# A decoder layer on one core: sums of weight tiles moved from VectorE to adding DMAs, and the work of T1 put first

## The chip, the cores and the metric

The kernel runs on one core of one Trainium2 chip. The metric is device time in microseconds, the median of the runs. The engines are TensorE (PE: matmuls and, as PEld, weight loads), VectorE (DVE), ScalarE (ACT), GpSimd (POOL) and SyncE (SP). Each runs its own list of instructions in order and waits for the others by semaphores. DMAs are issued here from SP's queue and POOL's; a DMA issued by POOL can add what it moves to what stands at the destination.

## The reference

One layer of a decoder trunk (DEPTH is 1, so the mixer is the pooling one): a norm, multi-scale causal pooling with a blockwise projection, a residual, a norm, and a gated feed-forward with a causal convolution of three taps. All in float32, sequence 1024, width 1024, hidden width 2816.

```python
def conv_ffn(x, w_in, conv_w, conv_b, w_out):
    h = causal_depthwise_conv(x @ w_in, conv_w, conv_b)
    val, gate = jnp.split(h, 2, axis=-1)
    return (jax.nn.silu(gate) * val) @ w_out

    h = rms_norm(x, norm_mix_g[layer])
    y = pool_mixer(h, pool_w[j], pool_b[j], pool_scale[j])
    x = x + y
    x = x + conv_ffn(rms_norm(x, norm_ffn_g[layer]), ...)
```

## The kernel before

**Stages.** First the mixer: eight tiles j of 128 rows are normed, pooled by matmuls (`psd`), projected (`psy`) and added to x. Each tile is normed again (`n2`), turned by TensorE in eight transposes (`pst`) and becomes a column block of the operands of the feed-forward. The second stage multiplies by `w_in`: 22 tiles n of 128 hidden units of the value and 128 of the gate. The third multiplies by `w_out`. It is not touched.

**Seven products instead of eight.** Both matrix products are done on two by two blocks with seven block products and some sums. For `w_in` one side is the weight tile `win` (blocks a11, a12, a21, a22), the other the turned rows (b11 to b22, kept in `n2f`). From the tile come S3 = a11 + a21, S1 = a21 + a22, S2 = a11 + S1 and S4 = a12 + S2, each in place of a block but S3, which has a buffer of its own. From the rows come T1 = b11 - b12, T3 = b22 - b12, T2 = -b22 - T1 and T4 = b22 - b21 + T1. The products are P1 = A11 B11, P2 = A12 B21, P5 = S1 T1, P3 = S4 B22, P6 = S2 T2, P7 = S3 T3, P4 = A22 T4.

**High and low parts.** Every operand is split: ScalarE rounds it into a high part (line 76 for weight tiles, line 311 for the rows' operands) and VectorE subtracts that from the source for the remainder (lines 77 and 312). A block product is twelve matmuls 128x512: for each of four slices of depth high by high, high by remainder, remainder by high. So the first matmul needs only the high parts, the second the rows' remainder too. The splits of one operand T2, T3, T4 or B22 come in two halves.

**Banks.** P1 and P2 of a tile add up in a bank X, P5 and P3 in a bank Z, and P6, P7 and P4 in a bank Y. Between them VectorE reads the bank: q2 after P6 (line 401), hb after P7 (line 409: r less Y), and hb's other half after P4 (line 414). r is read from Z after P5 (line 406). P4 may only add into Y once hb has been read. After P4 come the convolutions of value and gate (lines 419 to 421), a Silu and a product, and g goes to DRAM.

**Order.** The program is written as a list of events (n, P); while event k runs, the splits of event k + 5 are issued (`prep_event`). Tiles 0 and 1 take part in the mixer's last steps: P1 and P2 there, then P5, P3, P6, P7, P4. A scheduler places the instructions on each engine by its own estimates, with `tc.issue_after` as a constraint. The load of weight tile n + 2 (line 320) is issued once A22 of tile n is split. The sums of tiles 0 and 1 are made by POOL's adding DMAs (line 334), those of all later tiles by VectorE (lines 350 to 358).

## Time and profile before

| | |
|---|---|
| median of 3 runs | 704.09 us (703.36 to 705.65) |
| the profiled execution | 702.61 us, of which the span is 700.9 |
| TensorE busy | 693.9 us, 3154 matmuls |
| VectorE busy | 600.5 us |
| ScalarE busy | 343.2 us |
| GpSimd busy | 12.5 us |
| first matmul of P5 of tile 0 | 78.55 us |
| first matmul of P6 of tile 0 | 90.06 us |

In the profile's rows a tile has its name without its number (S is S3's buffer, T any of T1 to T4, B any of B11, B21, B22). A row of the timeline gives the start in the span, the length, the engine, the line, the operation, what is written and read, and the idle time before it with what ended it. A busy share is an average over the span: what a stage is worth is read from that stage.

### The profile page before, as it was taken

How to read it: one execution, taken by the hardware profiler on the slowest of the kernel's cores; microseconds unless marked ns; L12 is line 12 of the kernel's file. 1: busy time of each engine (PE TensorE's matmuls, PEld its weight loads, DVE VectorE, ACT ScalarE, POOL GpSimd, SP SyncE). 2: the span in 40 equal slices, each digit the busy share in tenths (PEclk: the TensorE clock that was granted, in tenths of full speed). 3: DMA queues.
4: the chain of work that ended last, by engine and by line, in shares of the span. 5: the costliest groups of instructions: out<-in, count | busy, mean ns of one | idle time of the engine just before them, and what ended most of it. 6: DMA issues, size and time to landing. Idle time of an engine off the chain costs nothing.

```text
span 700.9 us, 8493 instructions
## 1 busy us (share of the span) xinstructions
PE 693.9 (99%) x3154; PEld 573.7 (82%) x3154; DVE 600.5 (86%) x885; ACT 343.2 (49%) x515; POOL 12.5 (2%) x30
## 2 busy tenths in 40 slices
PE   8999999999999999999999999999999999999998
PEld 5898778888888888888888888888888888888886
DVE  5688999999888888888988888876887988999985
ACT  4786545454444444444545454454554444444431
POOL 3110000000000000000000000000000000000000
PEclk9999999999999999999999999999999999999999
DMA  9854112232222112222222212229989700122131
GB/s 307 302 141 121 57 65 91 89 122 91 67 84 74 60 78 90 91 90 91 91 90 91 86 65 91 91 84 338 335 305 335 277 22 1 61 90 87 64 106 60
DMA packets 32555, 85.47 MB, mean 122 GB/s; under 512 B 3689, under 2 KB 5377, under 8 KB 29698
## 3 DMA queue, kind: packets, MB, share of 16 engines
q1 hardware_dynamic: 31296, 82.82, 32.8%
...
q8 instruction: 24, 0.39, 0.2%
...
## 4 chain that ended last, share of the span: by engine, by line
PE 96%; DVE 2%; DMA 1%; ACT 1%; issue 0%; ACTq 0%; DVEq 0%
PE oP L723 30%; PE Y L372 26%; PE Z L372 17%; PE X L372 16%; PE psy L259 3%; PE psd L180 2%; DMA bias_hl<-rows_raw 1%; PE pst L292 1%; PE psy L262 1%; DVE n2f L323 0%; DMA x<-in_x_dram 0%; DVE T L312 0%; PE ps_edges L180 0%; PE ps_gain L227 0%; DVE n L277 0%; DVE S4s L77 0%
## 5 line engine op out<-in xcount | busy, mean ns | idle before, releaser
L723 PE MATMUL oP<-oBP,oAP 128*128 128x512 f32 (+1 forms) x924 | 208.8, 388 | 0.0
L723 PEld LDWEIGHTS oP<-oBP,oAP 128*128 128x128 f32 x924 | 172.9, 188 | 36.0 <-DVE oBP L77 0.3
L372 PE MATMUL Z<-T,S1s 128*128 128x512 f32 x264 | 64.0, 390 | 1.4 <-ACT T L311 1.2
L372 PE MATMUL X<-B,A11s 128*128 128x512 f32 x264 | 64.3, 390 | 0.0
L372 PE MATMUL Y<-T,S2s 128*128 128x512 f32 x264 | 64.0, 390 | 0.0
L372 PE MATMUL X<-B,A12s 128*128 128x512 f32 x264 | 63.5, 389 | 0.0
L372 PE MATMUL Y<-T,S3s 128*128 128x512 f32 x264 | 63.4, 389 | 0.0
L372 PE MATMUL Y<-T,A22s 128*128 128x512 f32 x264 | 63.4, 389 | 0.0
L372 PE MATMUL Z<-B,S4s 128*128 128x512 f32 x264 | 63.2, 389 | 0.0
L372 PEld LDWEIGHTS Z<-T,S1s 128*128 128x128 f32 x264 | 49.3, 188 | 12.6 <-ACT T L311 1.6
L372 PEld LDWEIGHTS Y<-T,S2s 128*128 128x128 f32 x264 | 49.4, 188 | 10.8 <-ACT S2s L76 0.4
L372 PEld LDWEIGHTS Y<-T,S3s 128*128 128x128 f32 x264 | 49.5, 188 | 10.3
L372 PEld LDWEIGHTS Z<-B,S4s 128*128 128x128 f32 x264 | 49.5, 188 | 10.3
L372 PEld LDWEIGHTS Y<-T,A22s 128*128 128x128 f32 x264 | 49.5, 188 | 10.3
L372 PEld LDWEIGHTS X<-B,A12s 128*128 128x128 f32 x264 | 49.5, 188 | 10.2
L372 PEld LDWEIGHTS X<-B,A11s 128*128 128x128 f32 x264 | 49.4, 188 | 10.2
L76 ACT ACTIVATE oBP<-blk 128x512 fp32r<-128x512 f32 x53 | 33.5, 633 | 49.1 <-PE oP L723 32.2
L77 DVE TENSOR_TENSOR oBP<-blk,oBP 128x512 fp32r<-128x512 f32 x53 | 36.6, 691 | 13.3 <-ACT oBP L76 13.3
L430 ACT ACTIVATE gate<-gate 128x1024 f32<-128x1024 f32 x22 | 23.3, 1061 | 44.5 <-DVE gate L421 44.5
L76 ACT ACTIVATE oAP<-blk 128x512 fp32r<-128x512 f32 x55 | 34.1, 621 | 19.2 <-DVE blk L323 15.9
L326 DVE TENSOR_TENSOR win<-win 128x512 f32<-128x512 f32 x60 | 41.3, 688 | 1.1
L77 DVE TENSOR_TENSOR oAP<-blk,oAP 128x512 fp32r<-128x512 f32 x55 | 37.7, 685 | 2.6 <-ACT oAP L76 2.6
(128 smaller groups left out, 941.4 us busy)
## 6 DMA issues: line engine op xcount, KB each, us to landing
win<-in_w_in_dram SPq DMA_DIRECT2D x22, 1024.0 KB, 4.8
...
```

Of the source, the lines that this page charges most:

```text
L76: nc.scalar.activation(t[:, 0, :], src, AF.Copy)
L77: m = nc.vector.tensor_tensor(t[:, 1, :], src, t[:, 0, :].bitcast(F32), ALU.subtract)
L180: m = nc.tensor.matmul(ps[:, c * P : (c + 1) * P], src[:, c * P : (c + 1) * P], weights[:, c // 2, :], start=True, stop=True)
L259: nc.tensor.matmul(o, dh[:, c, :], wps[:, c, :], start=c % 4 == 0, stop=False, skip_group_check=True)
L262: m = nc.tensor.matmul(ps[:, cols], ones, bias_hl[:, cols], start=False, stop=True, skip_group_check=True)
L292: nc.tensor.transpose(ps[:, c * P : (c + 1) * P], n2[:, c * P : (c + 1) * P], ident)
L326: nc.vector.tensor_tensor(out, a, b, ALU.add)
L372: nc.tensor.matmul(bank, a[:, i, ks], b[:, l, k, :], start=opens and m == 0, stop=m == 11, skip_group_check=not opens)
L430: nc.scalar.activation(gate, gate, AF.Silu)
L723: nc.tensor.matmul(bank, a[:, u, i * P : (i + 1) * P], b[:, v, c], start=opens and first, stop=g == NP2 - 1 and m == 2, skip_group_check=n ...
```

## The change

- T4's sum with T1 and the four sums of weight tiles 2, 3 and 4 are done by adding DMAs of POOL (`more`, `sums_in`, LATER_SUMS). A DMA from DRAM first fills S3's buffer with a11. T4's two adds move 512 KB each, the others 256 KB.
- The transposes of a row tile (`ffn_turn`) are apart from what is made of it (`ffn_operand`, `ffn_last`). For tiles 6 and 7 T1 is made first and T4's difference (`ffn_last`) follows r of tile 0. The last transposes stand at a fixed place, after the third slice of P2 of tile 0 (`between`). The norm of tile 7 stands ahead of the subtractions of tile 6.
- A tile `lower` is taken first in the pool of Y and Z, so that Z lies in other banks. B22's splits and r are issued sooner. The splits of events 7 to 9 follow r, and those of events 14 and 15 are held back.

```diff
@@ -285,13 +285,21 @@
     for b in ("B11", "T1", "B21"):
         nops[b] = nop_tile(nop_a, b)
 
-    def ffn_operand(j):
+    turned = {}
+
+    def ffn_turn(j):
         n2 = n2s.pop(j)
         ps = bank2(f"pst{j}")
         for c in range(NK):
-            nc.tensor.transpose(ps[:, c * P : (c + 1) * P], n2[:, c * P : (c + 1) * P], ident)
-        cols = slice(j * P, (j + 1) * P)
-        ps3 = ps.rearrange("p (c s) -> p c s", c=NK)
+            m = nc.tensor.transpose(ps[:, c * P : (c + 1) * P], n2[:, c * P : (c + 1) * P], ident)
+        marks["turned"] = m.ins
+        turned[j] = ps.rearrange("p (c s) -> p c s", c=NK)
+        if j >= NS // 2:
+            nc.scalar.activation(n2f[:, 4:, j * P : (j + 1) * P], turned[j][:, 4:, :], AF.Copy)
+        return m.ins
+
+    def ffn_operand(j, last=True):
+        ps3, cols = turned[j], slice(j * P, (j + 1) * P)
         lo, hi = slice(0, 4), slice(4, 8)
         if j < NS // 2:
             split_n(nops["B11"], ps3[:, lo, :], cols)
@@ -299,17 +307,23 @@
             nc.scalar.activation(n2f[:, :, cols], ps3, AF.Copy)
             return
         cols0 = slice(cols.start - NH, cols.stop - NH)
-        b11, b12, b21, b22 = n2f[:, lo, cols0], ps3[:, lo, :], n2f[:, hi, cols0], n2f[:, hi, cols]
-        nc.scalar.activation(b22, ps3[:, hi, :], AF.Copy)
+        b11, b12, b22 = n2f[:, lo, cols0], ps3[:, lo, :], n2f[:, hi, cols]
+
         sub(b11, b11, b12)
-        split_n(nops["T1"], b11, cols0)
-        sub(n2f[:, lo, cols], b22, b12)
-        sub(b21, b22, b21)
+        m = sub(n2f[:, lo, cols], b22, b12)
+        if last:
+            m = ffn_last(j)
+        with tc.issue_after(m):
+            marks[f"T1_{j}"] = split_n(nops["T1"], b11, cols0)
+
+    def ffn_last(j):
+        b21, b22 = (n2f[:, 4:, t * P : (t + 1) * P] for t in (j - NS // 2, j))
+        return sub(b21, b22, b21)
 
     def split_n(t, src, cols=slice(None), ks=slice(None)):
         h = t[:, 0, ks, cols]
-        nc.scalar.activation(h, src, AF.Copy)
-        nc.vector.tensor_tensor(t[:, 1, ks, cols], src, h.bitcast(F32), ALU.subtract)
+        marks["split_hi"] = nc.scalar.activation(h, src, AF.Copy).ins
+        return nc.vector.tensor_tensor(t[:, 1, ks, cols], src, h.bitcast(F32), ALU.subtract).ins
 
 
     order = [j + k * NP2 for j in range(NP2) for k in range(2)]
...
 
+    def more(out, a):
+        nc.gpsimd.dma_start(out, a, accum_op=ALU.add)
+
     def sums_in(n, step):
-
-        def more(out, a):
-            nc.gpsimd.dma_start(out, a, accum_op=ALU.add)
 
         a11, a12, a21, a22 = (raws[n][:, i, k * NH : (k + 1) * NH] for i in range(2) for k in range(2))
         if step == 0:
@@ -339,9 +353,10 @@
             nc.sync.dma_start(s3, w_in[order[n]][:, 0, :NH])
             more(s3, a21)
             more(a21, a22)
-        else:
+        if step in (1, "S2"):
             sums[n, "S2"] = a11
             more(a11, a21)
+        if step in (1, "S4"):
             sums[n, "S4"] = a12
             more(a12, a11)
 
@@ -361,16 +376,28 @@
         else:
             src = {"A11": a11, "A12": a12, "S1": a21, "A22": a22, "S2": a11, "S4": a12}[op]
         aops[n, op] = split(src, f"{op}s_{n}")
+        if n in LATER_SUMS and op in ("A11", "A12"):
+            sums_in(n, {"A11": "S2", "A12": "S4"}[op])
+
+            if op == "A12" and n + 1 in LATER_SUMS:
+                sums_in(n + 1, 0)
         if op == "A22" and n + 2 < NF:
             load_in(n + 2)
-
-    def product(bank, a, b, opens):
-        m = 0
+            if n + 2 == LATER_SUMS[0]:
+                sums_in(n + 2, 0)
+
+    def product(bank, a, b, opens, between):
+
+        m, order = 0, nullcontext()
         for k in range(4):
             ks = slice(k * P, (k + 1) * P)
-            for i, l in ((0, 0), (0, 1), (1, 0)):
-                nc.tensor.matmul(bank, a[:, i, ks], b[:, l, k, :], start=opens and m == 0, stop=m == 11, skip_group_check=not opens)
-                m += 1
+            with order:
+                for i, l in ((0, 0), (0, 1), (1, 0)):
+                    last = nc.tensor.matmul(bank, a[:, i, ks], b[:, l, k, :], start=opens and m == 0, stop=m == 11, skip_group_check=not opens)
+                    m += 1
+            if between and k == 2:
+                with tc.issue_after(last.ins):
+                    order = tc.issue_after(between())
 
     STEPS = {
         "P1": ("A11", "B11", "X"), "P6": ("S2", "T2", "Y"), "P5": ("S1", "T1", "Z"), "P2": ("A12", "B21", "X"),
...
@@ -493,11 +523,21 @@
             mixer_window(j - 1)
         if 1 <= j - 2 < NS:
             mixer_out(j - 2)
-        if 0 <= j - 2 < NS:
-            with tc.issue_after(marks["dh1+"]):
-                ffn_norm(j - 2)
-        if 0 <= j - 4 < NS:
-            ffn_operand(j - 4)
+        if j == 9:
+            ffn_turn(5)
+            with tc.issue_after(marks[7]):
+                ffn_operand(5)
+            with tc.issue_after(marks["T1_5"]):
+                ffn_norm(7)
+        elif j == 10:
+            ffn_turn(6)
+        else:
+            if 0 <= j - 2 < NS:
+                with tc.issue_after(marks["dh1+"]):
+                    ffn_norm(j - 2)
+            if 0 <= j - 4 < NS - 1:
+                ffn_turn(j - 4)
+                ffn_operand(j - 4)
         if j in (4, 6):
             load_in(j // 2 - 2)
             sums_in(j // 2 - 2, 0)
@@ -506,8 +546,19 @@
                 prep_event(j - 5)
         if j in (7, 8):
             sums_in(j - 7, 1)
-        if j in (8, 10, 11):
-            event((8, 10, 11).index(j))
+        if j == 8:
+            with tc.issue_after(marks["n2_6"]):
+                prep_event(4)
+                prep_event(5)
+            event(0)
+        if j == 10:
+            event(1)
+        if j == 11:
+            event(2, between=lambda: ffn_turn(7))
+            with tc.issue_after(marks["n2_7"]):
+                ffn_operand(6, last=False)
+                with tc.issue_after(marks["T1_6"]):
+                    ffn_operand(7, last=False)
         with tc.issue_after(marks["edges"]):
             stat(j + 1)
             stat(j + 2)
@@ -515,19 +566,29 @@
     nop_b = ctx.enter_context(tc.tile_pool(name="nop_b", bufs=1))
     left = ctx.enter_context(tc.tile_pool(name="left", bufs=1))
     ps_yz = ctx.enter_context(tc.tile_pool(name="ps_yz", bufs=3, space=PSUM))
+
+    ps_yz.tile([P, NH], F32, tag="Y", name="lower")
     for b in ("T2", "T3", "B22", "T4"):
         nops[b] = nop_tile(nop_b, b)
-    for k in range(4, 4 + LOOK):
-        with tc.issue_after(marks[NS - 1]):
-            prep_event(k)
     s0, s1 = slice(0, NH), slice(NH, S)
     lo, hi = slice(0, 4), slice(4, 8)
     halves = [slice(0, 2), slice(2, 4)]
     t1, t3, b22, t4 = n2f[:, lo, s0], n2f[:, lo, s1], n2f[:, hi, s1], n2f[:, hi, s0]
-    event(3)
-    event(4)
+    with tc.issue_after(marks["T1_7"]), tc.issue_after(marks["split_hi"]):
+        prep_event(6)
+        for ks in halves:
+            m = split_n(nops["B22"], b22[:, ks], ks=ks)
+    with tc.issue_after(marks["turned"]):
+        event(3)
+    with tc.issue_after(m):
+        event(4, prep=False)
+    with tc.issue_after(marks["r_0"]):
+        for j in (6, 7):
+            ffn_last(j)
+        for k in range(7, 4 + LOOK + 1):
+            prep_event(k)
     for ks in halves:
-        split_n(nops["B22"], b22[:, ks], ks=ks)
+        more(t4[:, ks], t1[:, ks])
     event(5)
     event(6)
     for ks in halves:
@@ -537,13 +598,17 @@
     event(8)
     for ks in halves:
         split_n(nops["T3"], t3[:, ks], ks=ks)
+    prep_event(9 + LOOK)
     for ks in halves:
-        add(t4[:, ks], t4[:, ks], t1[:, ks])
         split_n(nops["T4"], t4[:, ks], ks=ks)
     mid.close()
     late_stack = ExitStack()
     late = late_stack.enter_context(tc.tile_pool(name="late", bufs=1, side="right"))
-    for k in range(9, len(events)):
+    event(9, prep=False)
+    event(10, prep=False)
+    with tc.issue_after(marks["val0"][0]), tc.issue_after(marks["val0"][1]):
+        prep_event(10 + LOOK)
+    for k in range(11, len(events)):
         event(k)
     late_stack.close()
 
```

On VectorE the piece from r of tile 0 (`r_0`) to the first remainder of T2 read so before (line 534 makes T2; names end in the tile's number and a buffer number):

```order
L406 TENSOR_TENSOR r_0_832<-q1_0_673,Z0_819 128x512
L77 TENSOR_TENSOR A22s_0_838<-win0_415,A22s_0_838 128x512
L77 TENSOR_TENSOR S2s_1_858<-win1_540,S2s_1_858 128x512
L534 SCALAR_TENSOR_TENSOR n2f_161<-n2f_161 128x2x512
L406 TENSOR_TENSOR r_1_856<-q1_1_741,Z1_843 128x512
L534 SCALAR_TENSOR_TENSOR n2f_161<-n2f_161 128x2x512
L312 TENSOR_TENSOR T2_783<-n2f_161,T2_783 128x1024
```

and reads so now:

```order
L435 TENSOR_TENSOR r_0_826<-q1_0_679,Z0_813 128x512
L337 TENSOR_TENSOR n2f_161<-n2f_161 128x4x128 x2
L77 TENSOR_TENSOR S4s_1_830<-win1_540,S4s_1_830 128x512
L77 TENSOR_TENSOR S2s_0_833<-win0_415,S2s_0_833 128x512
L77 TENSOR_TENSOR S3s_0_836<-S3_0_417,S3s_0_836 128x512
L77 TENSOR_TENSOR A22s_0_841<-win0_415,A22s_0_841 128x512
L435 TENSOR_TENSOR r_1_863<-q1_1_742,Z1_850 128x512
L77 TENSOR_TENSOR S2s_1_865<-win1_540,S2s_1_865 128x512
L595 SCALAR_TENSOR_TENSOR n2f_161<-n2f_161 128x2x512 x2
L77 TENSOR_TENSOR S3s_1_886<-S3_1_542,S3s_1_886 128x512
L326 TENSOR_TENSOR T2_788<-n2f_161,T2_788 128x1024
```

Behind r_0 stand two subtractions for T4 (line 337), the splits of S4 of tile 1, of S2 and S3 of tile 0, which stood ahead of it before, and S3 of tile 1 stands ahead of T2's remainder.

Later on VectorE, from the remainder of S2 of tile 2 to the reading of bank Y of tile 1 after P7 (`hb1`), before:

```order
L77 TENSOR_TENSOR S2s_2_950<-win2_841,S2s_2_950 128x512
L414 TENSOR_TENSOR hb0_944<-q1_0_673,Y0_899 128x512
L77 TENSOR_TENSOR S1s_2_977<-win2_841,S1s_2_977 128x512
L401 TENSOR_TENSOR q2_1_993<-Y1_980,q1_1_741 128x512
L77 TENSOR_TENSOR A12s_2_996<-win2_841,A12s_2_996 128x512
L420 SCALAR_TENSOR_TENSOR gate22_970<-hb0_944,par_sb_121,gate22_970 128x1023
L403 TENSOR_TENSOR ha1_814<-Z1_843,q2_1_993 128x512
L421 SCALAR_TENSOR_TENSOR gate22_970<-hb0_944,par_sb_121,gate22_970 128x1022
L77 TENSOR_TENSOR S3s_2_1013<-S3_2_946,S3s_2_1013 128x512
L409 TENSOR_TENSOR hb1_1011<-r_1_856,Y1_980 128x512
```

and now (lines 449 and 450 are the taps of the convolutions):

```order
L77 TENSOR_TENSOR S2s_2_976<-win2_844,S2s_2_976 128x512
L450 SCALAR_TENSOR_TENSOR val0_965<-ha0_766,par_sb_121,val0_965 128x1022
L77 TENSOR_TENSOR S1s_2_979<-win2_844,S1s_2_979 128x512
L443 TENSOR_TENSOR hb0_950<-q1_0_679,Y0_906 128x512
L432 TENSOR_TENSOR ha1_811<-Z1_850,q2_1_995 128x512
L77 TENSOR_TENSOR A12s_2_998<-win2_844,A12s_2_998 128x512
L77 TENSOR_TENSOR S3s_2_1020<-S3_2_846,S3s_2_1020 128x512
L449 SCALAR_TENSOR_TENSOR gate22_969<-hb0_950,par_sb_121,gate22_969 128x1023
L449 SCALAR_TENSOR_TENSOR val11_1036<-ha1_811,par_sb_121,val11_1036 128x1023
L450 SCALAR_TENSOR_TENSOR gate22_969<-hb0_950,par_sb_121,gate22_969 128x1022
L450 SCALAR_TENSOR_TENSOR val11_1036<-ha1_811,par_sb_121,val11_1036 128x1022
L438 TENSOR_TENSOR hb1_1018<-r_1_863,Y1_982 128x512
```

The reading `hb1` stood ninth behind S2s of tile 2 and now stands eleventh; the splits among the rows are the same. The row `S2s_2` now waits for a DMA instead of for VectorE itself.

POOL's list ended with S4 of tile 1 before, and now goes on with these adds (`n2f` is T4's sum, `S3` the buffer of S3):

```order
L346 DMA n2f_161<-n2f_161 128x2x512 x2
L346 DMA S3_2_846<-win2_844 128x512
L346 DMA win2_844<-win2_844 128x512 x2
L346 DMA S3_3_1002<-win3_904 128x512
L346 DMA win3_904<-win3_904 128x512
L346 DMA win2_844<-win2_844 128x512
L346 DMA win3_904<-win3_904 128x512
L346 DMA S3_4_1142<-win4_1068 128x512
L346 DMA win4_1068<-win4_1068 128x512
L346 DMA win3_904<-win3_904 128x512
L346 DMA win4_1068<-win4_1068 128x512 x2
```

All these rows are new. They are issued in this order, each when its own inputs are there.

## The prediction

> **What bounds the kernel now.** I read the page first: the span, the busy times, and the chain that ended last by engine.

> ```profile
> span 700.9 us, 8493 instructions
> PE 693.9 (99%) x3154; PEld 573.7 (82%) x3154; DVE 600.5 (86%) x885; ACT 343.2 (49%) x515; POOL 12.5 (2%) x30
> PE 96%; DVE 2%; DMA 1%; ACT 1%; issue 0%; ACTq 0%; DVEq 0%
> ```

> TensorE is busy for 693.9 of 700.9 us and makes up 96% of the chain, so time can only be won where TensorE itself stands still. The chain in order of time shows where it does not. Its columns are start, length and what ran.

> ```profile
> 158.66 2.72 PE Z L372 x12
> ```

> From there up to the second stage one product of twelve matmuls follows the other every 2.72 us, 0.227 a matmul, and the change leaves those products as they are. After the first 60 us TensorE's timeline (start, length, count, and in brackets the idle time before it and its releaser) shows two waits for another engine:

> ```profile
> 75.01 2.33 PE L372 MATMUL X<-B,A12s 128*128 128x512 f32 x9
> 78.55 0.73 PE L372 MATMUL Z<-T,S1s 128*128 128x512 f32 x2 [1.21 <-ACT T L311]
> 79.51 5.27 PE L372 MATMUL Z<-T,S1s 128*128 128x512 f32 x22 [0.23 <-DVE T L312]
> 84.62 5.60 PE L372 MATMUL Z<-B,S4s 128*128 128x512 f32 x24
> 90.06 4.01 PE L372 MATMUL Y<-T,S2s 128*128 128x512 f32 x17
> ...
> 100.96 2.88 PE L372 MATMUL Y<-T,A22s 128*128 128x512 f32 x12
> 103.78 0.73 PE L372 MATMUL Y<-T,S2s 128*128 128x512 f32 x2
> 104.35 0.68 PE L372 MATMUL Z<-T,S1s 128*128 128x512 f32 x2
> 104.87 2.32 PE L372 MATMUL Y<-T,S2s 128*128 128x512 f32 x9
> 107.03 2.88 PE L372 MATMUL Y<-T,S3s 128*128 128x512 f32 x12
> ```

> The nine matmuls end at 77.34. The last of a group outlasts its 0.227 by 0.16 (0.39 long), so Z was due at 77.2 and started at 78.55: 1.4 late. The third matmul of Z was due at 79.0 and started at 79.51: 0.5. Around 104 us twelve matmuls take 2.82 instead of 2.72, and the next 13 take 3.25 instead of 2.95: 0.4. The 22 from 79.51 lose 0.1. **All that can be won is 2.4 us**, 0.34%. Behind TensorE stands VectorE; six windows of 12 us from 66 to 138, summed:

> ```profile
> sum 72.00, PE 70.56 PEld 57.30 DVE 71.44 ACT 40.35 POOL 0.00; mean PE 11.76 PEld 9.55 DVE 11.91 ACT 6.73 POOL 0.00
> ```

> It is busy for 71.44 of 72 us there. Whoever puts a wait into VectorE's queue in this stretch puts it, some instructions later, into TensorE.

> **The change part by part: T1.** VectorE's and ScalarE's rows here and below (start, length):

> ```profile
> 62.42 0.68 DVE L312 TENSOR_TENSOR T<-n2f,T 128x512 fp32r<-128x512 f32 x1
> 63.66 1.28 DVE L277 SCALAR_TENSOR_TENSOR n<-x,st_b,gain_b 128x1024 f32<-128x1024 f32 x1
> 66.37 1.22 DVE L265 TENSOR_TENSOR x<-psy,x 128x1024 f32<-128x1024 f32 x1 [1.42 <-PE psy L262]
> 72.77 1.28 DVE L277 SCALAR_TENSOR_TENSOR n<-x,st_b,gain_b 128x1024 f32<-128x1024 f32 x1
> 78.77 0.69 DVE L312 TENSOR_TENSOR T<-n2f,T 128x512 fp32r<-128x512 f32 x1
> ```

> ```profile
> 67.24 0.60 ACT L303 ACTIVATE n2f<-pst 128x512 f32<-128x512 f32 x1 [3.67 <-PE pst L292]
> 82.33 0.63 ACT L76 ACTIVATE S2s<-win 128x512 fp32r<-128x512 f32 x1 [3.31 <-PE Z L372]
> 111.65 1.06 ACT L430 ACTIVATE gate<-gate 128x1024 f32<-128x1024 f32 x1
> ```

> A 128x512 subtraction takes up 0.60 (82.33 to 82.93 in the rows further below). In the new order the two remainders of S1 fill the 1.42 us before the sum x of tile 7, which stays at 66.37 and takes 1.14. The three subtractions of transposed tile 5 wait for ScalarE's copy (67.24 + 0.60) and run from 67.9 to 69.7. T1's remainder and three one-column instructions follow (0.60, and 63.02 to 63.66, so 0.64; a fourth is hidden), and the norm of tile 7 starts at 71.0 instead of 72.77. TensorE turns it at 72.9, after nine matmuls, and is done at 73.8. ScalarE's copy ends at 74.5, the first subtraction at 75.2, T1's high part at 75.8, its remainder at 76.6. Z is due at 77.2, unchanged: 0.6 to spare. **Both stalls go, 1.9 us.** The 48 matmuls of Z (10.9 us) then end at 88.1, against 90.06 now. The 0.4 at 104 goes too, because the new order does not cut those groups up; the 0.1 with it.

> **What is late next: T2.**

> ```profile
> 82.33 0.69 DVE L406 TENSOR_TENSOR r<-q,Z 128x512 f32<-128x512 f32 x1
> 82.93 0.69 DVE L77 TENSOR_TENSOR A22s<-win,A22s 128x512 fp32r<-128x512 f32 x1
> 85.87 1.22 DVE L534 SCALAR_TENSOR_TENSOR n2f<-n2f 128x1024 f32<-128x1024 f32 x1
> 87.00 1.22 DVE L312 TENSOR_TENSOR T<-n2f,T 128x1024 fp32r<-128x1024 f32 x1
> ...
> 101.13 1.28 DVE L420 SCALAR_TENSOR_TENSOR val<-ha,par_sb,val 128x1023 f32<-128x1023 f32 x1
> 102.32 0.68 DVE L326 TENSOR_TENSOR win<-win 128x512 f32<-128x512 f32 x1
> ```

> VectorE computes r of tile 0 when Z's first twelve matmuls are done: 77.2 + 11 x 0.227 + 0.39, with 0.05 to wake, 80.1. Behind it now stand two subtractions for T4, S4s, S2s, S3s, A22s, r, S2s (with r nine at 0.60, 5.4), two at 1.13 and S3s: T2's remainder starts at 88.4 and ends at 89.6. Today the same row starts at 87.00 and TensorE comes for it at 90.06, so it costs nothing. After the change TensorE comes at 88.1, has two matmuls that need the high parts alone, and waits from 88.5: **plus 1.1**. This follows from counts between one point of TensorE and the next, and does not hang on how T1 goes.

> **The sums by DMAs.** T4's two additions (2.3 us) and twelve sums of weight tiles (7.2) leave VectorE. But each of the twelve becomes a wait of ScalarE and VectorE for a landing, and POOL issues them one after the other.

> ```profile
> 83.65 0.33 SPq L320 DMA_DIRECT2D win<-in_w_in_dram  x1
> ```

> ```profile
> win<-in_w_in_dram SPq DMA_DIRECT2D x22, 1024.0 KB, 4.8
> ```

> ```profile
> DMA to landing us min/median/max: 3.3/3.3/4.3
> ```

> ```profile
> DMA to landing us min/median/max: 3.8/4.1/4.3
> ```

> ```profile
> 31.76 1.20 POOL L334 DMA_DIRECT2D S<-win  x1
> 36.61 0.85 POOL L334 DMA_DIRECT2D win<-win  x1 [3.65 <-DMA S<-win]
> ```

> The load of weight tile 2 is issued when A22s is done (82.93 + 0.69, issue at 83.65) and lands 4.8 later. In the new order A22s starts at 80.1 + 6 x 0.60 = 83.7, so the tile lands at 89.2. An add lands 3.3 after its issue at best. The add issued at 31.76 landed 4.3 later (the longer of the two S adds), at 36.06, and the one that waited for it was issued at 36.61: 0.55 to wake. A link is 3.85. S3 needs one link, S1 waits for S3's, S2 for S1's: S2 lands at 89.2 + 3 x 3.85 = 100.8. ScalarE splits it (0.63), VectorE takes it at 101.5. VectorE had finished all that stands ahead of it at 100.0 (88.4 + seven instructions of 1.13 to 1.20 and six of 0.60): it idles 1.5 us. From it on stand six instructions of 0.60 and five conv taps of 1.19 before hb of tile 1 (0.68 long), so hb is done at 111.8. P4 of tile 1 adds into the bank that hb reads and cannot start before. TensorE comes for it 96 matmuls after 89.2, at 111.0: **plus 0.8**. Today the window view shows VectorE with no idle time to speak of here, so there is no such wait.

> The same happens a tile later. After hb VectorE needs 3.6 us to the remainder of A11 of tile 3 (four at 0.60, one at 1.13), at 115.3; only then may S2 of tile 3 be added: a link, three splits of some 0.52, a Silu of 1.06, a product and hb of tile 2 (1.13 and 0.68), 123.4 to 123.7. TensorE comes 48 matmuls after 111.8, at 122.7: **plus 0.8**. For tiles 3 and 4 I count nothing: VectorE saves 2.4 us a tile (four sums of 0.60), and by then that is more than it idles.

> [...]

> **Sharing of the transfer engines.** What each queue's packets took of the 16 engines, in a window of 8 us with one load of a weight tile, and in one with one add:

> ```profile
> q1 hardware_dynamic: 144, 1.05, 35.7%
> ```

> ```profile
> q0 software_dynamic: 144, 0.26, 19.1%
> ```

> A load takes 2.86 us of all engines and an add of 256 KB 1.53. T4's two adds are 512 KB each, 6.1 together, and are issued from 82.3 on (two subtractions after r); tile 2's load falls among them at 84.4, S3's add behind, and tile 3's load beside that. No row shows an add beside a load. Lower bound: the add yields nothing and S3 lands at 93.1. Upper bound: from 82.3, with 1.8 of start (3.3 less 1.53), 6.1 + 2.86 + 1.53 + 2.86 are served one by one, the S3 add last: 97.4. Between 0 and 4.3 late; I take the middle, **plus 2.1**, since both queues ask at the same time and nothing here says that one goes first. It goes through to P4 of tile 1 undiminished, as VectorE idles for it.

> [...]

> Other parts: the three early loads of 256 KB (S3 of tiles 2 to 4) wait behind nothing that TensorE needs, and the one before 30 us stands ahead of the stores of x alone; at most some 0.1. POOL's own queue holds nothing but these adds. B22 is ready by 80, three us before use.

> **Sum:** -2.4 + 1.1 + 0.8 + 0.8 + 2.1 = +2.4 us. The profiled execution took 702.61 us (span 700.9 and 1.7 around it), which makes 705.0; the median of the three runs is 1.5 above it, 704.09, so **706.5**. Its own range is 704.4 to 708.7 (sharing at 0 and 4.3).

> **Rivals.** 0.3% of this kernel, 2.1 us, is about what a measurement can tell from no change.
> (A) The forecast, 706.5, chance 0.46.
> (B) No sharing: -2.4 + 2.7, 704.4. For it: a load leaves many engine slices free; against: 13 us of transfers in 15 us. 0.22.
> (C) The adds keep up: from S2 landing by 100.0 on, P4 is never waited for, and T2's 1.1 alone is left: 702.8, or 703.6 if only tile 2's comes in time; not slower. It needs links 0.3 shorter than the shortest of the rows. [...] 0.12.
> (D) Every link is like the slowest add, 4.3: 1.0 more a link, three for tile 2, one each for tiles 3 to 5: 710. Seen once in eight adds, under load. 0.10.
> (E) Nothing waits, T2 included: 701.7. Against: the count above. 0.05.
> (F) T1 is not on time: the 0.6 to spare is used up by one more wait of VectorE for ScalarE, and up to 1 us of the old stall stays: 707. 0.05.

> Faster by over 0.3% (below 702.0): E, 0.05. Within (to 706.2): B, C and the lower edge of A, 0.39. Slower: the rest, 0.56. The range that leaves out E and D's upper part is 702.8 to 708.9.

> **What would show it.** T1: no idle time before Z at 77 us. T2: TensorE idle about 1.1 after two Y matmuls near 88.5, released by VectorE. Adds: VectorE idle before the remainder of S2s of tile 2 near 100, and TensorE idle before P4 of tiles 1 and 2, near 111 and 123. Sharing: loads of tiles 2 and 3 landing later than 4.8, adds later than 3.3. I would be wrong if TensorE had no gap at 111, or if gaps appeared past 150 us.

## The result, and the profile after

| | before | after |
|---|---|---|
| median | 704.44 us (703.36 to 705.65) | 714.12 us (713.81 to 714.63) |
| the profiled execution, span | 702.61, 700.9 | 714.24, 712.1 |

Four runs of each on one chip give a ratio of 1.0141, with an interval of 1.0124 to 1.0157: **9.7 us slower**. The direction was forecast, and +2.4 us of it; the time lies past the upper end of the stated range (708.9) and past the slowest rival (D, 710). One later run, of the kernel e2 below, took 2509.9 us and is in neither its median nor its ratio. The page's head, and the groups that TensorE waited for between 60 and 200 us (total, times, longest), after:

```profile
span 712.1 us, 8548 instructions
PE 697.3 (98%) x3154; PEld 575.2 (81%) x3154; DVE 592.7 (83%) x871; ACT 342.9 (48%) x515; POOL 24.9 (3%) x44
```

```profile
PE Y L396 <- DVE hb L438: 6.9, 2, 4.2
PE Y L396 <- DVE T L326: 1.0, 1, 1.0
PE Y L396 <- ACT S2s L76: 0.6, 1, 0.6
PE Y L396 <- DVE q L430: 0.3, 1, 0.3
```

VectorE is 7.8 us less busy than before (600.5) and GpSimd 12.4 more. Both waits for T1 are gone; four other kinds, five waits in all, stand in their place. TensorE's timeline, after:

```profile
78.41 5.60 PE L396 MATMUL Z<-T,S1s 128*128 128x512 f32 x24
...
89.29 0.61 PE L396 MATMUL Y<-T,S2s 128*128 128x512 f32 x2
90.90 5.10 PE L396 MATMUL Y<-T,S2s 128*128 128x512 f32 x21 [0.99 <-DVE T L326]
95.83 2.88 PE L396 MATMUL Y<-T,S3s 128*128 128x512 f32 x12
...
101.36 2.91 PE L396 MATMUL Y<-T,A22s 128*128 128x512 f32 x12
...
108.22 3.33 PE L396 MATMUL Y<-T,S2s 128*128 128x512 f32 x12 [0.55 <-ACT S2s L76]
111.38 2.89 PE L396 MATMUL Z<-T,S1s 128*128 128x512 f32 x12
118.52 4.60 PE L396 MATMUL Y<-T,A22s 128*128 128x512 f32 x12 [4.25 <-DVE hb L438]
122.95 2.88 PE L396 MATMUL X<-B,A12s 128*128 128x512 f32 x12
...
133.91 2.99 PE L396 MATMUL Y<-T,A22s 128*128 128x512 f32 x12 [2.63 <-DVE hb L438]
136.73 2.88 PE L396 MATMUL X<-B,A11s 128*128 128x512 f32 x12
```

The reading: from one start to the next, less 0.2267 for each matmul between, is what was lost there. With 23, 22, 27, 12, 12, 12, 36 and 12 matmuls between the rows from 89.29 on:

| where | lost, us | forecast |
|---|---|---|
| the start of the execution (below) | +1.4 | - |
| T1 (Y at 89.29 for 90.06, with the start 1.4 later), and the 0.4 at 104 us of before | -2.2 and -0.4 | -2.4 |
| T2 (89.29 to 95.83) | +1.3 | +1.1 |
| q (to 101.36) | +0.5 | - |
| S2 of tile 2 (to 111.38) | +1.2 | - |
| hb of tile 1 (to 118.52) | +4.4 | +0.8 and +2.1 |
| the twelve matmuls of P4 of tile 1 | +1.7 | - |
| hb of tile 2 (to 136.73) | +2.9 | +0.8 |
| sum, before rounding: so much later stands the last of these matmuls | +10.9 | +2.4 |

The start does not come from the change. The second block of pooling matmuls begins at 15.48 us in the profile before and at 16.89 in the one after, 1.4 later, and lasts 1.95 in both. The granted clock rises to full at 6.3 us in the one profile and at 9.4 in the other, and the four matmuls of `ps_scale`, the second group of TensorE, take 2.62 and 3.75 us, where four later ones of that shape (`ps_gain`) take 1.88 in both. In the profiles of e1, e2, e3 and e5 below, whose kernels begin like the kernel after, the same four take 1.96, 2.54, 2.07 and 1.96. The start thus differs from one profile to the next, and the medians need not have it: 10.9 less 1.4 is 9.5, against 9.7.

**The matmuls that took longer.** P4 of tile 1 takes 4.60 instead of 2.88. The windows view of it and of what follows (bounds, length, busy time and count of PE, PEld, DVE, ACT and POOL; the third number from the end is the granted clock):

```profile
118.70:122.10 3.40, 3.40 (x9) 2.63 (x9) 2.68 (x4) 1.64 (x2) 0.00 (x0) 0.50 0.39 82
122.20:125.60 3.40, 3.40 (x16) 2.80 (x16) 2.33 (x5) 1.25 (x1) 0.85 (x1) 1.00 0.98 364
```

For 3.4 us after the wait the clock is 0.50, with 9 matmuls begun instead of 16: 1.7 us on top of what the wait itself lasts.

**The chain to hb of tile 1.** SP's loads, POOL's adds, ScalarE's and VectorE's rows, after (the row of two loads covers the issue of tile 2's load at 85.66 and of tile 3's at 91.51; POOL's row of `n2f` has T4's two adds):

```profile
85.66 6.18 SPq L334 DMA_DIRECT2D win<-in_w_in_dram  x2
119.69 0.33 SPq L334 DMA_DIRECT2D win<-in_w_in_dram  x1
```

```profile
83.52 2.41 POOL L346 DMA_DIRECT2D n2f<-n2f  x2 [20.35 <-DVE n2f L337]
96.12 0.88 POOL L346 DMA_DIRECT2D S<-win  x1 [10.19 <-DMA win<-in_w_in_dram]
100.31 0.84 POOL L346 DMA_DIRECT2D win<-win  x1 [3.32 <-DVE T L326]
104.10 0.85 POOL L346 DMA_DIRECT2D win<-win  x1 [2.95 <-DMA win<-win]
...
123.33 0.85 POOL L346 DMA_DIRECT2D win<-win  x1 [9.72 <-DVE A11s L77]
```

```profile
95.67 0.63 ACT L76 ACTIVATE A11s<-win 128x512 fp32r<-128x512 f32 x1 [3.77 <-DMA win<-in_w_in_dram]
107.54 0.63 ACT L76 ACTIVATE S2s<-win 128x512 fp32r<-128x512 f32 x1 [6.36 <-DMA win<-win]
```

```profile
96.34 0.69 DVE L77 TENSOR_TENSOR A11s<-win,A11s 128x512 fp32r<-128x512 f32 x1 [0.89 <-ACT A11s L76]
108.20 0.69 DVE L77 TENSOR_TENSOR S2s<-win,S2s 128x512 fp32r<-128x512 f32 x1 [5.70 <-ACT S2s L76]
117.78 0.68 DVE L438 TENSOR_TENSOR hb<-r,Y 128x512 f32<-128x512 f32 x1
```

Tile 2's load is issued at 85.66 and lands at 95.6: 9.9 instead of 4.8. From S3's add to S1's is 4.2, from S1's to S2's 3.8, and S2 lands 3.3 after its issue. VectorE stands still for 5.7 us before the remainder of S2s, and then has eleven instructions without a pause up to hb. What the 16 transfer engines did is shown by two windows, 85.5 to 88.5 and 89.5 to 93.5 us (q1 is the loads' queue and q0 POOL's; packets, MB, share of the engines), and by the two adds that took longest:

```profile
q0 software_dynamic: 288, 0.56, 113.8%
```

```profile
q1 hardware_dynamic: 123, 0.99, 62.3%
q0 software_dynamic: 131, 0.27, 39.5%
```

```profile
n2f<-n2f POOLq DMA_DIRECT2D x1, 512.0 KB, 11.7
```

```profile
win<-win POOLq DMA_DIRECT2D x1, 256.0 KB, 5.9
```

In the first window the load has been issued, yet only POOL's queue moves anything: T4's first add runs to its end at 88.2, and the second begins. The load's first packet comes at 89.4, 3.7 after its issue, where a load in the kernel before has it 1.0 after. In the second window load and T4's second add move about as many packets, 123 and 131. Why the load's first packet comes only behind T4's first add the trace does not say.

The last row is the add of S2 of tile 3, and hb of tile 2 stands behind it. It is issued at 123.33, behind the load of tile 4 (119.69) and the store of g (512 KB, 121.63), and takes 5.9 instead of 3.3. By the record of the packets the load has moved its last at 124.3, before the add's first at 125.0. What runs beside the add is the store, up to 127.5, and two fetches of instructions, 1.0 and 0.7 us long, from 125.0 on. In the record of this trace an add ends with 16 packets of 4 bytes. Fifteen of this add's are there by 127.45, and the sixteenth comes at 128.96: some 1.5 of the 2.6 us hang on that last one. That each of the 16 engines sends one of them, so that a single engine was late, is an estimate from the count.

### The profile page after: what moved, and what is told of

Same layout as the page of the kernel before. It is cut to its first block, busy times and chain, and to the rows that moved or that the text cites. A ratio compares the mean times of both kernels' runs of the same rounds, so it can differ in the third digit from the quotient of the medians.

```text
span 712.1 us, 8548 instructions
## 1 busy us (share of the span) xinstructions
PE 697.3 (98%) x3154; PEld 575.2 (81%) x3154; DVE 592.7 (83%) x871; ACT 342.9 (48%) x515; POOL 24.9 (3%) x44
## 4 chain that ended last, share of the span: by engine, by line
PE 81%; ACT 0%; issue 0%; DVE 0%; DVEq 0%
PE oP L788 29%; PE Y L396 22%; PE X L396 15%; PE Z L396 15%; PE rest L788 0%; ACT gate L460 0%; DVE hb L438 0%; ACT A12s L76 0%; DVE z L340 0%; DVE val L461 0%; DVEq L449 0%
## 5 line engine op out<-in xcount | busy, mean ns | idle before, releaser
L396 PE MATMUL Y<-T,A22s 128*128 128x512 f32 x264 | 65.3, 397 | 6.9 <-DVE hb L438 6.9
L396 PEld LDWEIGHTS Y<-T,S3s 128*128 128x128 f32 x264 | 49.5, 188 | 10.9 <-DVE q L430 0.7
L396 PEld LDWEIGHTS Z<-T,S1s 128*128 128x128 f32 x264 | 49.5, 188 | 10.3
L396 PEld LDWEIGHTS Z<-B,S4s 128*128 128x128 f32 x264 | 49.6, 188 | 10.3
L76 ACT ACTIVATE oBP<-blk 128x512 fp32r<-128x512 f32 x53 | 33.5, 633 | 49.1 <-PE oP L788 32.2
L77 DVE TENSOR_TENSOR oBP<-blk,oBP 128x512 fp32r<-128x512 f32 x53 | 36.7, 692 | 13.3 <-ACT oBP L76 13.3
L76 ACT ACTIVATE oAP<-blk 128x512 fp32r<-128x512 f32 x55 | 34.1, 621 | 19.2 <-DVE blk L337 15.9
L77 DVE TENSOR_TENSOR oAP<-blk,oAP 128x512 fp32r<-128x512 f32 x55 | 37.7, 686 | 2.6 <-ACT oAP L76 2.6
L449 DVE SCALAR_TENSOR_TENSOR val<-ha,par_sb,val 128x1023 f32<-128x1023 f32 x22 | 28.2, 1284 | 14.0 <-ACT val L448 13.8
## 6 DMA issues: line engine op xcount, KB each, us to landing
win<-in_w_in_dram SPq DMA_DIRECT2D x22, 1024.0 KB, 4.8
```

Of the source, the lines that this page charges most:

```text
L76: nc.scalar.activation(t[:, 0, :], src, AF.Copy)
L77: m = nc.vector.tensor_tensor(t[:, 1, :], src, t[:, 0, :].bitcast(F32), ALU.subtract)
L396: last = nc.tensor.matmul(bank, a[:, i, ks], b[:, l, k, :], start=opens and m == 0, stop=m == 11, skip_group_check=not opens)
L449: marks["taps"] = nc.vector.scalar_tensor_tensor(t[:, 1:], src[:, : S - 1], w[1], t[:, 1:], op0=ALU.mult, op1=ALU.add).ins
```

## Experiments

Each is a change to the kernel after, unless it says otherwise. Ratios are to the kernel before, run in turns on the same chip. Line numbers in the rows are those of the kernel run.

**Which part costs the time.** T4's sum back on VectorE (e1), the sums of tiles 2 to 4 back on VectorE (e2), both back (e3, which leaves T1's part alone), and T4's sum by DMAs in the kernel before (e13).

```diff
 e1, e3:
-    for ks in halves:
-        more(t4[:, ks], t1[:, ks])
     event(5)
...
     for ks in halves:
+        add(t4[:, ks], t4[:, ks], t1[:, ks])
         split_n(nops["T4"], t4[:, ks], ks=ks)
 e2, e3:
-    LATER_SUMS = (2, 3, 4)
+    LATER_SUMS = ()
 e13, to the kernel before:
+    for ks in halves:
+        nc.gpsimd.dma_start(t4[:, ks], t1[:, ks], accum_op=ALU.add)
     event(5)
...
-        add(t4[:, ks], t4[:, ks], t1[:, ks])
```

> T4's sum is back on VectorE, as in the kernel before; the sums of weight tiles 2 to 4 stay DMAs that add. Theory 1 (T4's two adds of 512 KB hold the transfer engines, and the load of weight tile 2 gets its first packet only when the first add is through): the load lands 4.8 us after its issue again and not 9.9, S2 of tile 2 lands near 102 instead of 107.5, TensorE's wait for hb of tile 1 falls from 4.25 to between 0 and 2.7 (VectorE has 2.3 us of T4's additions back), the half clock behind it is gone, and the time is 706 to 709 us. Theory 2 (the chain of three adds is too long by itself, T4 is beside the point): S2 still lands after 105, the wait stays above 3.4 us, and the time is 711 to 714.

> The sums of weight tiles 2 to 4 are back on VectorE; T4's sum stays two DMAs that add. Theory 1 (the waits come from a chain of adds that starts with a late load): without the chain the late load costs at most the 0.9 us that VectorE idled for A11s of tile 2 and no wait for hb is left; the wait for T2 (1.2) stays; 702.5 to 705. Theory 2 (the chain is at fault, T4 beside the point): the same time, and the load lands 4.8 after its issue, T4's adds or not. Theory 3 (T4's adds themselves are too late for P4 of tile 0): a wait before P4 of tile 0 near 101 us, 705 to 708.

> Both sums are back on VectorE: only the new order round T1, the banks of Z and the transposes are left of the change. By the working of the prediction: the stall before Z near 77 us is gone (1.9 won), the 0.5 round 104 too, T2 comes late (1.1 to 1.3 lost), and VectorE has its 9.5 us back and is full from 78 to 140. 703 to 705 if that costs nothing else; 705 to 707 if VectorE, now without slack, is late for hb once more. The start: after's full clock came 3.2 us later than before's in the profiled executions; if that belongs to the order of the kernel, it is seen here again (1.4 us).

> The kernel before with one part of the change alone: T4's sum as two DMAs that add. The load of weight tile 2 lands 9 to 11 us after its issue, as it does in after. Theory 1 (a late load costs only where a chain hangs on it): VectorE wins 2.3 us, T1's stalls stay, and the time is 703.3 to 705 (no change). Theory 2 (T4's second add, 12 us from issue to landing in after, is too late for P4 of tile 0): a wait before P4 of tile 0 near 101 us and 705 to 708.

| | T4's sum | later sums | median, us | ratio | TensorE waits for |
|---|---|---|---|---|---|
| e3 | VectorE | VectorE | 708.13 | 1.0058 (1.0039 to 1.0076) | T2 1.0, val 0.9, q 2.0 and 1.0 |
| e2 | DMA | VectorE | 705.90 | 1.0028 (1.0015 to 1.0042) | T2 1.0, val 0.9, q 0.6 and 1.2 |
| e1 | VectorE | DMA | 712.18 | 1.0110 (1.0080 to 1.0139) | T2 1.0, hb 1.5 and 3.2, q 1.2 and 0.3 |
| after | DMA | DMA | 714.12 | 1.0141 (1.0124 to 1.0157) | T2 1.0, q 0.3, S2s 0.6, hb 4.2 and 2.6 |
| e13 | DMA | VectorE, old order | 703.50 | 0.9992 (0.9976 to 1.0008) | T1 1.2 and 0.2, as before |

So by the medians the later sums' DMAs cost some 4 us with T4's sum on VectorE and some 8 with T4's DMAs; T4's DMAs win some 2 where the later sums stay on VectorE and lose some 2 where they don't, but there the intervals overlap. The larger share of the time is the later sums, and the two kinds of DMA do worse together. In the old order T4's DMAs change nothing that the interval shows: the 2.3 us that they take from VectorE were hidden.

And T1's part by itself (e3) makes the kernel 3.9 us slower, although its two waits are gone in e1, e2 and e3 alike. In e3 the window of the longest wait, and all six from 66 to 138 us summed:

```profile
102.00:114.00 12.00, 10.02 (x37) 7.73 (x36) 12.00 (x16) 7.97 (x10) 0.00 (x0) 0.86 0.00 0
...
sum 72.00, PE 67.16 PEld 54.39 DVE 68.49 ACT 39.27 POOL 0.00; mean PE 11.19 PEld 9.07 DVE 11.41 ACT 6.54 POOL 0.00
```

While TensorE waits for q, VectorE is busy for all of the 12 us; two sums of tile 2 and reads of Y stand ahead of q in its list. Over the six windows TensorE is busy for 3.4 us less than in the kernel before (70.56). VectorE stands still for 3.5 us there, in some eight short waits for ScalarE and TensorE (0.5 of them before hb of tile 0, 1.3 at 117): with the products in this order it has to wait for its own operands, and what it loses so it cannot make up.

e1 was to show the chain without T4's adds. It shows that the 9.9 us of tile 2's load were their doing: here the load lands 5.0 after its issue. But S3's add then goes out at 89.81, just before the load of tile 3 at 90.14, and takes 7.3 to land. The longest wait lies elsewhere, and 6.8 us of half clock go with it. TensorE's row, VectorE's and ScalarE's:

```profile
148.63 5.46 PE L396 MATMUL Y<-T,A22s 128*128 128x512 f32 x12 [3.25 <-DVE hb L438]
```

```profile
143.46 0.69 DVE L340 TENSOR_TENSOR S<-win 128x512 f32<-128x512 f32 x1 [2.67 <-DMA win<-in_w_in_dram]
...
146.59 0.69 DVE L77 TENSOR_TENSOR S2s<-win,S2s 128x512 fp32r<-128x512 f32 x1 [1.71 <-ACT S2s L76]
```

```profile
145.93 0.63 ACT L76 ACTIVATE S2s<-win 128x512 fp32r<-128x512 f32 x1 [5.91 <-DMA win<-win]
```

VectorE's own first sum of tile 5 had been scheduled ahead of hb of tile 3 and waited for its load. But VectorE stands still once more behind it, for S2s of tile 4, and that wait ends last. Its add went out at 140.72, behind the load of tile 5 (137.81) and the store of g (139.02), and landed 5.2 after. The time came out as the rival theory had it, but not because a chain of three is too long by itself: again an add met other transfers.

**The half clock.** Fourteen matmuls into an unused bank, ahead of P4 of tile 1, so that TensorE doesn't stand still there (e4).

```diff
+    w = ps_yz.tile([P, NH], F32, tag="Z", name="warm")
+    with tc.issue_after(marks["product"]):
+        for m in range(14):
+            mm = nc.tensor.matmul(w, nops["T1"][:, 0, 0, :P], nops["T1"][:, 0, 0, :], start=m == 0, stop=m == 13)
+    with tc.issue_after(mm.ins):
+        event(13, prep=False)
```

> The kernel after, with 14 more matmuls (3.2 us) into a bank that nobody reads, between Z of tile 2 and P4 of tile 1, where TensorE stood idle for 4.25 us before the clock fell to a half for 3.4 us. VectorE's order changes a little there: the planner puts hb of tile 1 one tap earlier. Theory (the idle time itself brings the half clock): TensorE is idle for under 1.5 us before P4 of tile 1, no half clock follows, P4's twelve matmuls take 2.9 us and not 4.6, and the time is 1.5 to 2.5 us less than after's 714.1. Rival (the clock falls there whatever TensorE does): the half clock is still there and the time is within 0.6 us of 714.1 or above it.

714.79 us, ratio 1.0149 (1.0134 to 1.0164): no gain. TensorE's rows, and a window on what follows the second wait:

```profile
118.65 3.02 PE L396 MATMUL Y<-T,A22s 128*128 128x512 f32 x12 [0.93 <-DVE hb L439]
...
132.77 4.56 PE L396 MATMUL Y<-T,A22s 128*128 128x512 f32 x12 [2.93 <-DVE hb L439]
```

```profile
133.30:136.60 3.30, 3.30 (x9) 2.60 (x8) 1.96 (x4) 0.89 (x2) 0.00 (x0) 0.50 0.87 238
```

P4 of tile 1 now runs at full clock (3.02), so the half clock did come from TensorE standing still. But the 1.7 us are lost again one tile later, where a wait of 2.93 is followed by half clock, while in the kernel after a wait of 2.63 was not.

**Order and spacing of the transfers.** Tile 2's load ahead of T4's adds (e7); besides, tile 3's load held back (e8); besides, T2 moved up (e9).

```diff
 e7, e8, e9:
     with tc.issue_after(marks["r_0"]):
+        prep_event(10)
         for j in (6, 7):
             ffn_last(j)
+        for ks in halves:
+            marks["t4"] = more(t4[:, ks], t1[:, ks])
+        with tc.issue_after(marks["t4"]):
+            sums_in(2, 0)
...
-    for ks in halves:
-        more(t4[:, ks], t1[:, ks])
-    event(5)
+    event(5, prep=False)
 e8, e9:
-    event(8)
+    event(8, prep=False)
...
     with tc.issue_after(marks["val0"][0]), tc.issue_after(marks["val0"][1]):
+        prep_event(8 + LOOK)
         prep_event(10 + LOOK)
...
```

> The kernel after, with VectorE's A22s of tile 0 moved to the place right behind r of tile 0, so that the load of weight tile 2 is issued some 2.5 us earlier and before T4's two adds. Theory 1 (whichever transfer reaches the engines first is served, the other waits): the load lands 4.8 to 5.5 us after its issue, T4's adds come behind it, S2 of tile 2 lands 3 to 5 us earlier than in after (102.5 to 104.5 against 107.5), the wait before P4 of tile 1 is under 1.5 us, the half clock is gone, and the time is 706.5 to 710. Theory 2 (the sum of the bytes in that stretch decides, whatever the order): S2 lands after 106 and the time is 712 to 714.

> As the run before (the load of tile 2 ahead of T4's adds), and A22s of tile 1 is made some 10 us later on VectorE, so that the load of weight tile 3, which took the place of tile 2's adds in the engines, is issued only after val of tile 0, when S2's add of tile 2 is under way. Theory 1: the chain of tile 2 runs at 3.8 us a link as the prediction had it, S2 lands at 101 to 102.5, the waits before P4 of tiles 1 and 2 are 0 to 1 us each, T2's 1.0 stays, and the time is 704.5 to 707. Theory 2 (the sum of the bytes): above 709.

> As the run before, and VectorE makes T2 ahead of S3, of r of tile 1 and of S2 of tile 1 (the last differences stay ahead of it, since they read B22 before T2 overwrites it). Theory: T2's wait of 1.0 goes and 0.8 to 1.3 us with it: 703.5 to 706. Rival: the products that come instead wait for what was put behind T2 (r or S2 of tile 1), and the time is that of the run before within 0.5 us.

714.32, 714.47 and 714.38 us; ratios 1.0147 (1.0132 to 1.0162), 1.0158 (1.0129 to 1.0187) and 1.0133 (1.0087 to 1.0178). In e7 tile 2's load lands 6.9 after its issue, 5 us earlier than in the kernel after. The gain goes at once to the next link: S3's add, issued at 90.91, meets tile 3's load (89.99) and the rest of T4's second add, which lands at 96.4:

```profile
S<-win POOLq DMA_DIRECT2D x1, 256.0 KB, 7.9
```

S2's add then goes out at 103.13 instead of 104.10, and TensorE waits 4.29 before P4 of tile 1. With tile 3's load held back (e8) S3's add still takes 5.4 beside T4's second add, and the chain collides with the load two links later, at S2's add. SP and POOL in e8:

```profile
100.60 0.33 SPq L334 DMA_DIRECT2D win<-in_w_in_dram  x1
```

```profile
101.48 0.85 POOL L346 DMA_DIRECT2D win<-win  x1 [3.80 <-DMA win<-win]
```

That add landed 5.4 after its issue. Three orders of the same transfers thus give one time: no order among those tried gets the adds past two loads of 1 MB in this stretch. This is the time that the theory of the sum of the bytes gave; that one unlucky load was to blame falls. e9's interval is wide, and its wait for T2 stays.

**Both parts apart, and the transfers kept apart.** T4's sum on VectorE, tile 3's load held back, tile 5's sums behind hb of tile 3 (e10); besides, T2 moved up (e11).

```diff
+            with tc.issue_after(marks["hb_3"]):
+                add(s3, a11, a21)
+                add(a21, a21, a22)
...
-            add(s3, a11, a21)
-            add(a21, a21, a22)
...
```

> Chain without company: T4's sum is on VectorE, the load of weight tile 3 is held back until val of tile 0 (it goes out near 103 us), the sums of weight tiles 2 to 4 stay DMAs that add, and VectorE's first sum of tile 5 is put behind hb of tile 3 (in the run with T4 on VectorE it stood ahead of it and waited for the load). Theory 1 (the adds are late because other transfers hold the engines): S3, S1 and S2 of tile 2 land 3.0 us after each issue, 3.4 to 3.8 from issue to issue, S2 lands by 101, no wait of more than 0.5 us is left before P4 of tile 1, no half clock; what stays is T2's 1.0; 702 to 705 us. Theory 2 (a chain of three adds is too long by itself): S2 after 103, a wait of over 1.5 us before P4 of tile 1, 707 or more.

> As the run before, and T2 ahead of S3, of r of tile 1 and of S2 of tile 1 on VectorE. Theory: T2's wait of 1.0 goes; 701 to 704, below the kernel before. Rival (VectorE is full there in any order): the products after it wait for S2 or r of tile 1 for as long, and the time is that of the run before within 0.5.

707.39 us, 1.0052 (1.0035 to 1.0069), and 708.87, 1.0068 (1.0044 to 1.0092). In e10 S3's, S1's and S2's adds of tile 2 go out at 90.95, 95.21 and 99.02 and land 3.7, 3.3 and 3.3 later, and TensorE waits for nothing before P4 of tile 1 (T2's 1.0 stays): the chain alone, undisturbed, does come in time. In e11 the wait for T2 stays as well. In e10 the collision has moved to tiles 3 and 4. TensorE, and the windows behind its two waits:

```profile
138.76 3.02 PE L397 MATMUL Y<-T,S3s 128*128 128x512 f32 x12 [1.96 <-DVE q L431]
...
165.40 4.61 PE L397 MATMUL Y<-T,A22s 128*128 128x512 f32 x12 [1.82 <-DVE hb L439]
```

```profile
138.80:142.10 3.30, 3.30 (x15) 2.72 (x16) 1.39 (x3) 0.00 (x0) 0.84 (x1) 1.00 0.87 310
...
165.50:168.70 3.20, 3.20 (x9) 2.55 (x10) 2.44 (x4) 1.49 (x2) 0.00 (x0) 0.58 0.01 3
```

S2's add of tile 3 goes out at 118.89, the load of tile 4 at 118.02; S2's add of tile 4 at 139.83, the load of tile 5 at 136.92 and a store of g at 138.13. The two adds take 5.9 and 5.5, and VectorE stands still for 3.1 and 3.5 us behind them. This is built into the order of VectorE's list: S2's add of tile n follows the remainder of A11 of tile n, the load of tile n + 1 follows that of A22 of tile n - 1, and here these two start 0.6 and 2.4 us apart.

**T2 earlier.** With all sums on VectorE, T2's two halves ahead of the last differences (e5; since T2 overwrites B22, its T4 is made from other numbers), and with T4's sum by DMAs, behind them (e6).

```diff
 e5:
     with tc.issue_after(marks["r_0"]):
+        prep_event(7)
+        prep_event(8)
+        for ks in halves:
+            nc.vector.scalar_tensor_tensor(b22[:, ks], b22[:, ks], -1.0, t1[:, ks], op0=ALU.mult, op1=ALU.subtract)
+            split_n(nops["T2"], b22[:, ks], ks=ks)
+        prep_event(9)
         for j in (6, 7):
             ffn_last(j)
...
```

> As the run before (both sums on VectorE), and VectorE does the two halves of T2 ahead of the last differences and of S3, A22 and r. Theory (T2's wait comes from what stands ahead of it on VectorE): no wait for T2 near 90 us, 1.0 to 1.3 us less than the run before. Rival (VectorE is full in any order): the wait comes back at T3, at P4 of tile 0 or at hb of tile 1, and the time is the same within 0.5 us.

> T4's sum by DMAs, the sums of tiles 2 to 4 on VectorE (as in the run that had 706.2), and T2 ahead of S3, r of tile 1 and S2 of tile 1 on VectorE. Theory (T2's wait comes from what stands ahead of it): no wait for T2 near 90 us, 704.5 to 705.5. Rival (what is put behind it is waited for instead): 706 to 707.

707.82 us, 1.0057 (1.0034 to 1.0079): like e3. T2's wait is gone in e5, but r comes 0.4 late, hb 0.6 and q 2.3 instead of 2.0. e6 gives 705.81, 1.0029 (1.0018 to 1.0039), like e2: the scheduler put P6 of tile 0 ahead of P3 of tile 1 once T2 was ready sooner, so TensorE came sooner and waited 1.0 again. Whatever VectorE does first there, something else is late.

**All those sums left out.** If VectorE is what takes T1's gain back, the order after must be faster than the order before when VectorE has less to do. T4's sum and the sums of tiles 2 to 4 are left out of the kernel after (e14) and of the kernel before (e16), so that the products are made of other numbers, in unchanged shapes.

```diff
 e14:
-            more(s3, a21)
-            more(a21, a22)
+            if n < 2:
+                more(s3, a21)
+                more(a21, a22)
...
 e16, to the kernel before:
-            add(a11, a21, a11)
+            if n not in (2, 3, 4):
+                add(a11, a21, a11)
...
```

> The kernel after with T4's sum and the sums of weight tiles 2 to 4 left out altogether, on VectorE and as DMAs (so S1 to S4 and T4 are made from the unsummed operands): the change as it would be if the adding DMAs cost nothing. Theory 1 (T1's gain of 2.2 to 2.6 us is real, and VectorE's full queue took it back in the run with both sums on VectorE, 3.9 us above the kernel before): with 9.5 us less on VectorE only T2's wait of 1.0 is left, no half clock, 701.5 to 703.5. Theory 2 (the new order itself is slower, whatever VectorE has to do): waits before P4 of tile 0 and for q stay, 706 or more.

> The kernel before with the same sums left out (T4's and those of weight tiles 2 to 4; the operands are then unsummed). Theory 1: TensorE's stalls at T1 (1.9) stay, since they come from the norm of tile 7 and not from VectorE's load, only the 0.4 round 104 goes: 703 to 704, and the kernel after without sums is 1 to 2 us below it. Theory 2: the new order is slower by itself, and this kernel is below the other one by 2 us or more.

702.17 us, 0.9987 (0.9974 to 1.0001), and 702.75, 0.9992 (0.9982 to 1.0002). The one wait that is left in e14, and its six windows from 66 to 138 us:

```profile
PE Y L399 <- DVE T L326: 1.0, 1, 1.0
```

```profile
sum 72.00, PE 71.03 PEld 58.75 DVE 68.06 ACT 42.66 POOL 0.00; mean PE 11.84 PEld 9.79 DVE 11.34 ACT 7.11 POOL 0.00
```

Each against its own runs of the kernel before, e14 stands at -1.2 us and e3 at +3.9, and the programs differ in these sums and three loads of 256 KB alone, though the scheduler may place the rest differently; e16 keeps before's two waits for T1. So the sums in VectorE's list are what T1's order pays with. Without them the order wins, by the medians, about what the forecast gave it, T2's wait included (-2.4 + 1.1); the interval just reaches no change. Whether e14 beats e16 the intervals do not say.

**The adds as GpSimd's own instructions** instead of DMAs, T4's among them (e17) or on VectorE (e18).

```diff
-        nc.gpsimd.dma_start(out, a, accum_op=ALU.add)
+        nc.gpsimd.tensor_tensor(out, out, a, ALU.add) if by_pool else nc.gpsimd.dma_start(out, a, accum_op=ALU.add)
...
+            more(s3, a21, n >= 2)
...
```

> The kernel after with the same sums in the same places, but as additions that POOL itself computes (tensor_tensor) and not as DMAs that add: T4's two of 128x1024 and tiles 2 to 4's twelve of 128x512. No transfer, no landing, no load in the way. No run here shows POOL's time for one. Theory (the change fails only through the adding DMAs): as in the run without sums, T2's wait of 1.0 is left and at most a short one, 701.5 to 704, as fast as the kernel before or faster, provided a 128x512 addition takes POOL under 2.5 us, since three in a row have to be done before S2 of tile 2 is wanted at 101. Rival (POOL's additions and VectorE's hold each other up): VectorE's 128x512 subtractions take longer than 0.60 from start to start beside them, and the time is above 705.

> As the run before, with T4's sum on VectorE again (tiles 2 to 4 on POOL). Theory: VectorE has 2.3 us more before 100 us; a wait before P4 of tile 0 of under 1 us comes back, 702.5 to 705. Rival as before: above 706.

714.03 us, 1.0140 (1.0123 to 1.0156), and 710.89, 1.0100 (1.0083 to 1.0117). VectorE and POOL in e17:

```profile
83.08 2.88 DVE L77 TENSOR_TENSOR S2s<-win,S2s 128x512 fp32r<-128x512 f32 x1
85.89 2.83 DVE L77 TENSOR_TENSOR S3s<-S,S3s 128x512 fp32r<-128x512 f32 x1
```

```profile
82.65 5.52 POOL L346 TENSOR_TENSOR n2f<-n2f 128x1024 f32<-128x1024 f32 x2 [20.14 <-DVE n2f L337]
94.19 5.50 POOL L346 TENSOR_TENSOR S<-S,win 128x512 f32<-128x512 f32 x1 [6.02 <-DMA win<-in_w_in_dram]
```

The remainders of S2 and S3 take 2.88 and 2.83 while POOL makes T4's two halves; in e18, where POOL does nothing there, they take 0.69 each. TensorE then waits 4.0 for r. There VectorE loses 4.3 beside the sums that take 2.3 off it. At 94.19 it is POOL that is late: its sum S3 takes 5.50, where those from 104 us on take 1.3 to 2.2, and TensorE's waits for hb come to 3.8. In e18 they come to 3.9.

## Why the prediction was right in direction, and wrong in size

**T1: right.** Z starts without a wait, 2.2 us were won there and 0.4 at 104 us; forecast 2.4 for both.

**T2: right.** The wait stands where it was forecast, after two Y matmuls, released by VectorE: 0.99 idle, 1.3 lost, forecast 1.1. It was read from counts of instructions alone.

**The links: right.** 4.2, 3.8 and 3.3 to the landing, forecast 3.85, 3.85 and 3.3; from the remainder of S2s of tile 2 to the end of hb of tile 1 10.26, forecast 10.3. So rival C falls, and so does D's 4.3 for each add, where the add meets no other transfer. T2's wait rules out E, and Z without a wait F. The shortest add of the trace after takes 3.3 too.

**The sharing: the step that failed first.** The term was +2.1, the middle of 0 and 4.3; it measured 5.5. The forecast had S2s of tile 2 at 103.6 with the middle and at 105.8 with the upper bound. TensorE and VectorE stood 1.2 later than the forecast's base by then (Z at 78.41 instead of 77.2), which makes 104.8 and 107.0. Measured: 108.20, 3.4 later than the value taken and 1.2 past the upper bound. "Both queues ask at the same time" was wrong in effect, since T4's adds had the engines to themselves until the load's first packet at 89.4. And the upper bound was none: it counted one start of 1.8 us for transfers served one by one, but S3's add cannot be issued before the load has landed, so that POOL's waking (0.5) and the add's own start (1.4) come on top. Rival B, no sharing, falls with it.

**Where the 3.4 us appear.** Not at hb alone. With the load late, the remainder of A11 of tile 2 waits 0.9 at VectorE, ahead of q; and TensorE waits for the first part of S2s of tile 2: q's 0.5 and S2's 1.2 are, with 0.2 more at T2, 1.9 us, which the forecast counted at nothing, and the rest is hb of tile 1, 4.4 instead of 2.9. (T2's 0.2 has nothing to do with the load.)

**The half clock: not in the forecast.** It cost 1.7 us behind the wait for hb of tile 1. The forecast priced a wait by its length alone and put what follows it at nothing.

**hb of tile 2: right mechanism, mis-sized.** 2.9 instead of 0.8. The add took 5.9: beside it ran the store of g and two fetches of instructions, and neither is among the transfers that the forecast counted. "For tiles 3 and 4 I count nothing" holds: in the kernel after no wait is left past 140 us. But the two surpluses (3.4 and 2.1), the half clock (1.7) and T1's 0.2 to the other side make 7.0 of the 7.3 us between forecast and medians.

**What the forecast did not ask** is whether T1's gain lasts. It read that VectorE was busy for 71.44 of 72 us and drew the right conclusion for waits put into its queue, but not that a TensorE 2.4 us earlier meets the same full queue. e3 shows it: the gain is lost to the waits for T2, val and q and the half clock behind q, and 3.9 us more. In the kernel after, the sums are off VectorE, so this is not where its time went; it is why taking the DMAs back does not give the forecast gain either.

**What stays open.** How much of e3's loss is VectorE's work and how much the order in which the scheduler placed it was not told apart. Nor was a kernel run without the store of g or the fetches beside the add of tile 3, so that their part in its 5.9 us is read from the packets alone. No kernel run here is faster than the kernel before by more than the intervals.
